# The four-block sum of a Strassen part formed ahead of the part's last z, converted in halves, and VectorE's weight work tied into an order of need

## The chip, the cores and the metric

The program runs on one core of one Trainium2 chip. The metric is the device time of one execution in microseconds (us). Five engines matter: TensorE (PE in the profile; PEld is its weight load), VectorE (DVE), ScalarE (ACT), GpSimd (POOL) and SyncE (SP), which issues most transfers.

## What is computed

A decoder trunk of two layers over 512 positions of width 1024. Each layer has a mixer and then the block that this change is about, a gated convolution block:

```python
def conv_ffn(h, w_in, conv_w, conv_b, w_out):
    z = causal_dwconv(h @ w_in, conv_w, conv_b)
    u, g = jnp.split(z, 2, axis=-1)
    return (jax.nn.gelu(g) * u) @ w_out
...
    for l in range(DEPTH):
        ...
        h = rms_norm(x, norm_ffn[l])
        x = x + conv_ffn(h, ffn_w_in[l], ffn_conv_w[l], ffn_conv_b[l], ffn_w_out[l])
```

The inner width is 2816, that is 22 tiles of 128 channels, each with a gate g and a value u.

## The kernel before

**Precision.** Every product is made of three float32r products: each operand is split into a high part (rounded copy) and a low part (the rest). For weights, ScalarE copies the raw weight `wraw` into `whi`, and VectorE subtracts, `wlo = wraw - whi`; `convert` (L256 to L278) does that, four of each being kept (`WB`), three raw tiles (`RAW`). `mm3` then runs `whi` by `yh`, `whi` by `yl`, `wlo` by `yh`, in that order.

**Parts.** A feed-forward block runs in three parts, `PARTS`: 8, 8 and 6 of its 22 tiles. In a part, TensorE first makes the up-projections (tile `up`, 24 matmuls of 512 columns each, g and u in turn for each tile); VectorE scales each result into `z` (L807), ScalarE and VectorE apply the convolution (`a`, L810, L812), ScalarE the GELU (`gg`), and VectorE multiplies into `y` (L828). Then comes the part's down-projection (tile `dn`), added into the residual tiles `X`.

**Strassen in the down-projection.** The two parts of 8 tiles in each layer, four in all, use seven products instead of eight (matmuls of 128x256). Their left operands are blocks of the weight for a pair of output tiles `dp` (0 to 3): `a` (plain blocks, raw tile `wraw`), `s` and `r` (sums, tiles `ws` and `wr`) and `b` (a plain block, `wb`). `stage` loads blocks of a pair into `ws`, `wr`, `wb` by SP, and adds further blocks on the way with accumulating transfers issued by POOL. `form` finishes the sums on VectorE: the two-block sum half of `s` (L251), and from it and `wraw` the four-block sum, the other half of `r` (L253). The right operands are `y`, differences of its blocks (`tt`) and their high and low parts `yh`, `yl` (L311, L846, L847).

**Order.** TensorE follows `PORDER`, written out by hand; a step such as `"30"` is product 3 of pair 0, 12 matmuls (`20-` is the first 9 of them and `20+` the last 3). Below, "step 30" is that entry. `LEFT` says which left operand a product uses: 1 and 2 the halves of `a`, 5 and 6 those of `s`, 3 and 7 those of `r` (3 the four-block sum), 4 `b`. `WORDER` is the order in which left operands are converted. After each product its result is added to or taken from `X` on VectorE (L910, L908; products 5, 7 and 4 subtract). Products 6, 7 and 4 of a pair go on accumulating in the bank of product 1, so step 40 cannot begin before VectorE has read out step 70.

`wnext` converts `AHEAD` = 3 items ahead of the one in use, so a part's last up-projection starts with a0, s0 and a1 under way, and r0 is formed at the first down step. `behind` orders two instructions on an engine without a wait. `hold` keeps weight work of ScalarE and VectorE behind the split of the part's last `y`, so r0's four-block sum and both its conversions come after it. The scheduler that places instructions decides the rest of each engine's order; each engine runs its queue strictly in that order.

Of the kernel before, what the change touches and what calls it, by code (L numbers as in the profile page):

```python
# [17 lines left out]
P = 128  # L18
# [56 lines left out]
LEFT = {1: ("a", 0), 2: ("a", 1), 5: ("s", 0), 6: ("s", 1), 3: ("r", 0), 7: ("r", 1), 4: ("b", 0)}  # L75
WORDER = "a0 s0 a1 r0 s1 b0 a2 r1 s2 b1 a3 r2 s3 b2 r3 b3".split()
BANK = {1: "mm", 6: "mm", 7: "mm", 4: "mm", 5: "s", 3: "s", 2: "tr"}
# [5 lines left out]
def tile_trunk(ctx: ExitStack, tc: tile.TileContext, xT, par, fpar, w_v, w_q, w_k, w_u, w_pool, w_po, w_ao,  # L83
# [130 lines left out]
    sums = {}  # L214
    last_split, hold = [None, None], [None, None]

# [20 lines left out]
    def form(kind, i):  # L237
        n = chunks[i][1]
        h = n // 2
        stage(i)  # L240
        s, r, b = sums[i]
        if kind == "a":
            follow = [k for k in pairs if k > i]
            if follow and pairs[i][2] < KD // 2 - 1:
                stage(min(follow))
            return raw_of(i), n
        if kind == "b":
            return b[:, :h], h
        a = raw_of(i)
        if kind == "s":  # L250
            behind(nc.vector.tensor_tensor(s[:, h:n], s[:, :h], a[:, :h], op=ALU.add), hold[1])  # L251
            return s[:, :n], n
        behind(nc.vector.tensor_tensor(r[:, :h], s[:, h:n], a[:, h:], op=ALU.add), hold[1])  # L253
        return r[:, :n], n

    def convert():  # L256
        kind, at = items[len(ready)]
        if kind != "plain":
            raw, n = form(kind, at)
            hi, lo = (wp.tile([P, 1024], F32R, name=t, bufs=WB)[:, :n] for t in ("whi", "wlo"))  # L260
            behind(nc.scalar.copy(hi, raw), hold[0])  # L261
            behind(nc.vector.tensor_tensor(lo, raw, f(hi), op=ALU.subtract), hold[1])  # L262
            ready.append((hi, lo, n))
            return
        n = chunks[at][1]
# [6 lines left out]
        for i in range(parts):  # L272
# [3 lines left out]
            if len(ready) == 2:  # L276
                early[:] = [h_, l_]
        ready.append((hi, lo, n))  # L278

    def wnext(n, ahead=AHEAD):  # L280
# [519 lines left out]
    def ffn(layer, norm, after, cuts=None):  # L800
        def conv(m):
            c0 = (layer * 2 * NF + m) * 4
# [3 lines left out]
            z = T("z")  # L806
            ins = nc.vector.tensor_tensor(z, ps, bc, op=ALU.mult)  # L807
            later_ops[1] = later_ops[1] or ins
            a = T("a")
            nc.scalar.activation(a, z, AF.Identity, scale=cw[2], bias=cw[3])  # L810
            for sh, w in ((1, cw[1]), (2, cw[0])):
                nc.vector.scalar_tensor_tensor(a[:, sh:], z[:, :S - sh], w, a[:, sh:], op0=ALU.mult, op1=ALU.add)  # L812
            return a
# [5 lines left out]
    def part(j0, n, strassen, conv, after, cuts):  # L819
        def big(tag, w, dt=F32):  # L820
            return cur["tp"].tile([P, w], dt, name=tag, tag=tag, bufs=cur["bufs"][tag])

        def gated(j, y):
            g = conv(NF + j)
            gg = T("gg")
            nc.scalar.activation(gg, g, AF.Gelu_apprx_tanh)  # L826
            u = conv(j)
            nc.vector.tensor_tensor(y, u, gg, op=ALU.mult)  # L828
# [19 lines left out]
        for i in range(half):  # L848
# [16 lines left out]
            if late:  # L865
                sub(t1, b[0], b[1])
                cut_of(t1, 3, 4)
            gated(j0 + 2 * i + 1, y[:, S:])
            cut_of(y[:, S:], 1, 3)
# [16 lines left out]
        for what in PORDER:  # L886
# [3 lines left out]
            while key not in left:  # L890
                left[todo.pop(0)] = wnext(None)
            wh, wl = left[key]
            whole, fresh = what[-1] not in "+-", not what.endswith("+")
            if m in (1, 5, 2) and fresh:
# [9 lines left out]
            for d, t in {1: ((0, h0),), 2: ((0, h0),), 5: ((1, h1),), 6: ((0, h1),), 3: ((0, h1),), 7: ((1, h1),),  # L904
                         4: ((1, h0),)}[m]:
                x = X[2 * dp + d][:, t]
                if d:
                    nc.vector.tensor_tensor(x, x, ps, op=ALU.subtract)  # L908
                else:
                    nc.vector.tensor_tensor(x, ps, x, op=ALU.add)  # L910
        pe["on"] = False
# [187 lines left out]
```

## Time and profile before

| | us |
|---|---|
| median of 3 runs (1076.84 to 1077.23) | 1076.91 |
| the profiled execution | 1078.23 |
| its span, first to last instruction | 1076.5 |
| TensorE busy in the span | 1065.2 |
| VectorE busy | 835.1 |
| ScalarE busy | 545.6 |
| granted TensorE clock, mean | 1.000 |

The profiled execution took 1.32 us longer than the median of the runs, and 1.7 us of its time lie outside its span. The busy shares overlap: TensorE is busy in 99% of the span, VectorE in 78%, ScalarE in 51%.

### The profile page before, as it was taken

Reading aid. Unit: us, or ns where it says so; the run is one execution under the profiler, and the core shown is the slowest. Engines: PE = TensorE matmul, PEld = TensorE weight load, DVE = VectorE, ACT = ScalarE, POOL = GpSimd, SP = SyncE. Lnnn points to the kernel's source line nnn. Section 1 sums busy time; section 2 is a strip of 40 time slices with the busy share of each in tenths; the row PEclk is TensorE's granted clock in tenths of the full one; section 3 lists DMA queues with packets and bytes.
Section 4 is the critical chain, followed back from the end, with each engine's and each line's share of the span. In section 5 each row is a group of like instructions: output and inputs, shape, how many; then the busy total and the mean of one; then the engine's idle time right before and its main releaser. Section 6 shows DMA issues by size and latency. Waiting matters only on the chain.

```text
span 1076.5 us, 14242 instructions
## 1 busy us (share of the span) xinstructions
PE 1065.2 (99%) x5456; PEld 907.7 (84%) x5456; DVE 835.1 (78%) x1278; ACT 545.6 (51%) x785; POOL 46.6 (4%) x62
## 2 busy tenths in 40 slices
PE   9999999999999999999999999999999999999998
PEld 7888888888998889888888888888888888898887
DVE  7678879988868898676787989568898678976762
ACT  6557766544434444444648895445444344434440
POOL 1031001000100000000000000010001000000000
PEclk9999999999999999999999999999999999999999
DMA  7232115532762315322333133375317632144222
GB/s 265 97 101 85 62 57 154 140 98 59 184 172 97 97 42 136 119 87 75 122 98 108 50 103 87 104 212 141 98 40 196 175 96 85 57 118 134 84 75 81
DMA packets 41893, 118.09 MB, mean 110 GB/s; under 512 B 4832, under 2 KB 5216, under 8 KB 41824
## 3 DMA queue, kind: packets, MB, share of 16 engines
q1 hardware_dynamic: 36432, 107.47, 31.5%
q0 software_dynamic: 4608, 8.39, 5.0%
q10 hardware_dynamic: 784, 1.31, 0.5%
q8 instruction: 43, 0.70, 0.3%
q14 instruction: 26, 0.21, 0.1%
HBM read 114.01 MB, written 2.10 MB: 108 GB/s over the span
## 4 chain that ended last, share of the span: by engine, by line
PE 96%; DVE 1%; DMA 1%; ACT 1%; issue 0%; SPq 0%; DVEq 0%
PE up L299 44%; PE dn L299 25%; PE tk L299 6%; PE xr L299 5%; PE gt L299 5%; PE po L299 2%; PE u L299 2%; PE ao L299 2%; PE gp L299 1%; PE av L299 1%; PE s L299 1%; PE tr L302 1%; DMA ws<-in_dram 1%; DVE wlo L262 0%; ACT whi L261 0%; PE tp L302 0%
## 5 line engine op out<-in xcount | busy, mean ns | idle before, releaser
L299 PE MATMUL up<-xl,whi 128*128 128x512 f32 x704 | 274.0, 389 | 0.0
L299 PE MATMUL up<-xh,whi 128*128 128x512 f32 x704 | 273.9, 389 | 0.0
L299 PE MATMUL up<-xh,wlo 128*128 128x512 f32 x704 | 273.9, 389 | 0.0
L274 ACT CAST whi<-wraw 128x1024 fp32r<-128x1024 f32 (+4 forms) x177 | 165.6, 941 | 153.8 <-PE up L299 56.0
L275 DVE TENSOR_TENSOR wlo<-wraw,whi 128x1024 fp32r<-128x1024 f32 (+4 forms) x177 | 193.4, 1096 | 34.0 <-ACT whi L274 32.0
L299 PE MATMUL dn<-yh,whi 128*128 128x256 f32 (+1 forms) x550 | 166.4, 303 | 3.5 <-ACT whi L261 2.5
L299 PE MATMUL dn<-yh,wlo 128*128 128x256 f32 (+1 forms) x550 | 165.2, 301 | 3.0 <-DVE wlo L262 3.0
L299 PE MATMUL dn<-yl,whi 128*128 128x256 f32 (+1 forms) x550 | 164.8, 300 | 0.0
L299 PEld LDWEIGHTS up<-xl,whi 128*128 128x128 f32 x704 | 132.1, 188 | 27.5
L299 PEld LDWEIGHTS up<-xh,whi 128*128 128x128 f32 x704 | 132.1, 188 | 27.4
L299 PEld LDWEIGHTS up<-xh,wlo 128*128 128x128 f32 x704 | 132.1, 188 | 27.3
L812 DVE SCALAR_TENSOR_TENSOR a<-z,fprm,a 128x510 f32<-128x510 f32 (+1 forms) x176 | 130.9, 747 | 2.4
L807 DVE TENSOR_TENSOR z<-up,rbc 128x512 f32<-128x512 f32 x88 | 60.4, 688 | 68.0 <-PE up L299 67.7
L299 PEld LDWEIGHTS dn<-yh,whi 128*128 128x128 f32 x550 | 105.1, 191 | 9.1 <-ACT whi L261 3.4
L299 PEld LDWEIGHTS dn<-yh,wlo 128*128 128x128 f32 x550 | 105.1, 191 | 7.3 <-DVE wlo L262 3.9
L299 PEld LDWEIGHTS dn<-yl,whi 128*128 128x128 f32 x550 | 105.1, 191 | 3.7
L311 ACT CAST yh<-y 128x512 fp32r<-128x512 f32 (+1 forms) x44 | 23.9, 543 | 116.5 <-DVE y L828 116.5
L810 ACT ACTIVATE a<-z,fprm 128x512 f32<-128x512 f32 x88 | 71.4, 814 | 9.9 <-DVE z L807 8.9
L826 ACT ACTIVATE gg<-a 128x512 f32<-128x512 f32 x44 | 27.8, 633 | 81.2 <-DVE a L812 76.8
L299 PE MATMUL dn<-yy,whi 128*128 128x512 f32 x160 | 49.2, 389 | 0.0
L233 POOL DMA_DIRECT2D ws<-in_dram x16 | 14.3, 893 | 756.0 <-DMA wr<-in_dram 376.9
L416 DVE TENSOR_TENSOR x<-dn,x 128x512 f32<-128x512 f32 (+1 forms) x23 | 15.4, 668 | 36.2 <-PE dn L299 36.2
(218 smaller groups left out, 1656.6 us busy)
## 6 DMA issues: line engine op xcount, KB each, us to landing
wraw<-in_dram SPq DMA_DIRECT2D x147, 512.0 KB, 3.5
wraw<-in_dram SPq DMA_DIRECT2D x16, 384.0 KB, 3.1
wraw<-in_dram SPq DMA_DIRECT2D x16, 320.0 KB, 2.8
ws<-in_dram SPq DMA_DIRECT2D x16, 256.0 KB, 3.3
wr<-in_dram SPq DMA_DIRECT2D x16, 256.0 KB, 4.0
wb<-in_dram SPq DMA_DIRECT2D x16, 256.0 KB, 4.0
ws<-in_dram POOLq DMA_DIRECT2D x16, 256.0 KB, 6.2
wr<-in_dram POOLq DMA_DIRECT2D x16, 256.0 KB, 4.9
```

The lines of the kernel that those rows point to most:

```text
L233: nc.gpsimd.dma_start(out=s[:, :h], in_=low[:, h:], accum_op=ALU.add)
L274: h_ = nc.scalar.copy(hi[:, c], raw[:, c])
L275: l_ = nc.vector.tensor_tensor(lo[:, c], raw[:, c], f(hi[:, c]), op=ALU.subtract)
L299: in_order(nc.tensor.matmul(*a, **k))
L302: in_order(nc.tensor.transpose(*a))
L311: last_split[:] = [nc.scalar.copy(hi, src), nc.vector.tensor_sub(lo, src, f(hi))]
L416: nc.vector.tensor_tensor(X[d][:, t], ps[:, t], X[d][:, t], op=ALU.add)
L807: ins = nc.vector.tensor_tensor(z, ps, bc, op=ALU.mult)
L810: nc.scalar.activation(a, z, AF.Identity, scale=cw[2], bias=cw[3])
L812: nc.vector.scalar_tensor_tensor(a[:, sh:], z[:, :S - sh], w, a[:, sh:], op0=ALU.mult, op1=ALU.add)
L826: nc.scalar.activation(gg, g, AF.Gelu_apprx_tanh)
```

## The change

In the last u tile of a Strassen part, `two_halves` forms r0's four-block sum on VectorE ahead of that tile's `z` (L295 of the new code), converts its first half (which step 30 needs) right after `z`, ScalarE's part ahead of `a` (L299, L300), and leaves the second half's high part to ScalarE behind `a` (L308) and its low part (L313, `rest_low`) to a place behind the read-out of step 60. There a2 and b0 follow, then the second half of s1's low part, whose first half is made at step 50 (`convert(whole=False)`). a2 and b0 change places in `WORDER`. Steps 10, 50, 11 and 30 get an `ahead` of their own, and step 11 starts the load of a2 and the staging of pair 3. `form` no longer holds the sums behind the split of `y`; two-block sums of pairs 2 and 3 are tied behind the low part of their own `a` instead. TensorE's order is unchanged: the same matmuls, in the same sequence.

```diff
--- before.py
+++ after.py
@@ -73,7 +73,7 @@
 QB = {1: 0, 2: 1, 3: 2, 5: 3, 7: 4, 6: 5, 4: 6}
 
 LEFT = {1: ("a", 0), 2: ("a", 1), 5: ("s", 0), 6: ("s", 1), 3: ("r", 0), 7: ("r", 1), 4: ("b", 0)}
-WORDER = "a0 s0 a1 r0 s1 b0 a2 r1 s2 b1 a3 r2 s3 b2 r3 b3".split()
+WORDER = "a0 s0 a1 r0 s1 a2 b0 r1 s2 b1 a3 r2 s3 b2 r3 b3".split()
 BANK = {1: "mm", 6: "mm", 7: "mm", 4: "mm", 5: "s", 3: "s", 2: "tr"}
 
 PORDER = "10 50 11 20- 21- 20+ 21+ 30 60 51 70 12 40 61 31 22 71 52 41 13 62 32 23 72 53 63 42 73 33 43".split()
@@ -212,7 +212,7 @@
         raws.append(raw)
 
     sums = {}
-    last_split, hold = [None, None], [None, None]
+    last_split, hold, low_a = [None, None], [None, None], {}
 
     def raw_of(i):
         while len(raws) <= i:
@@ -248,20 +248,25 @@
             return b[:, :h], h
         a = raw_of(i)
         if kind == "s":
-            behind(nc.vector.tensor_tensor(s[:, h:n], s[:, :h], a[:, :h], op=ALU.add), hold[1])
+            behind(nc.vector.tensor_tensor(s[:, h:n], s[:, :h], a[:, :h], op=ALU.add), low_a.get(i))
             return s[:, :n], n
-        behind(nc.vector.tensor_tensor(r[:, :h], s[:, h:n], a[:, h:], op=ALU.add), hold[1])
+        nc.vector.tensor_tensor(r[:, :h], s[:, h:n], a[:, h:], op=ALU.add)
         return r[:, :n], n
 
-    def convert():
+    def convert(prev=None, whole=True):
         kind, at = items[len(ready)]
         if kind != "plain":
             raw, n = form(kind, at)
             hi, lo = (wp.tile([P, 1024], F32R, name=t, bufs=WB)[:, :n] for t in ("whi", "wlo"))
             behind(nc.scalar.copy(hi, raw), hold[0])
-            behind(nc.vector.tensor_tensor(lo, raw, f(hi), op=ALU.subtract), hold[1])
+            c = n if whole else n // 2
+            ins = behind(nc.vector.tensor_tensor(lo[:, :c], raw[:, :c], f(hi[:, :c]), op=ALU.subtract), prev or hold[1])
+            if kind == "a" and pairs[at][2] > 1:
+                low_a[at] = ins
             ready.append((hi, lo, n))
-            return
+            if not whole:
+                return lambda b: behind(nc.vector.tensor_tensor(lo[:, c:], raw[:, c:], f(hi[:, c:]), op=ALU.subtract), b)
+            return ins
         n = chunks[at][1]
         raw = raw_of(at)
         if n == S and "shi" in cur["bufs"]:
@@ -276,6 +281,36 @@
             if len(ready) == 2:
                 early[:] = [h_, l_]
         ready.append((hi, lo, n))
+
+    rest = []
+
+    def two_halves():
+
+
+        kind, at = items[len(ready)]
+        assert kind == "r"
+        n = chunks[at][1]
+        h = n // 2
+        _, r, _ = sums[at]
+        total = nc.vector.tensor_tensor(r[:, :h], sums[at][0][:, h:n], raw_of(at)[:, h:], op=ALU.add)
+
+        def finish(z):
+            hi, lo = (wp.tile([P, 1024], F32R, name=t, bufs=WB)[:, :n] for t in ("whi", "wlo"))
+            high = nc.scalar.copy(hi[:, :h], r[:, :h])
+            low = behind(nc.vector.tensor_tensor(lo[:, :h], r[:, :h], f(hi[:, :h]), op=ALU.subtract), z)
+            ready.append((hi, lo, n))
+            rest[:] = [hi[:, h:], lo[:, h:], r[:, h:n]]
+            return high, low
+
+        return total, finish
+
+    def rest_high(prev):
+        behind(nc.scalar.copy(rest[0], rest[2]), prev)
+
+    def rest_low(prev):
+        hi, lo, raw = rest
+        rest[:] = []
+        return behind(nc.vector.tensor_tensor(lo, raw, f(hi), op=ALU.subtract), prev)
 
     def wnext(n, ahead=AHEAD):
         while len(ready) < min(used[0] + 1 + ahead, len(items)):
@@ -798,18 +833,23 @@
 
 
     def ffn(layer, norm, after, cuts=None):
-        def conv(m):
+        def conv(m, ahead=None):
             c0 = (layer * 2 * NF + m) * 4
             cw = [fprm[:, c0 + i:c0 + i + 1] for i in range(4)]
             ps = up_tile(norm, "up")
             bc = norm.bc
             z = T("z")
-            ins = nc.vector.tensor_tensor(z, ps, bc, op=ALU.mult)
+            total, finish = ahead() if ahead else (None, None)
+            ins = behind(nc.vector.tensor_tensor(z, ps, bc, op=ALU.mult), total)
             later_ops[1] = later_ops[1] or ins
+            high, low = finish(ins) if ahead else (None, None)
             a = T("a")
-            nc.scalar.activation(a, z, AF.Identity, scale=cw[2], bias=cw[3])
+            ins = behind(nc.scalar.activation(a, z, AF.Identity, scale=cw[2], bias=cw[3]), high)
+            if ahead:
+                rest_high(ins)
             for sh, w in ((1, cw[1]), (2, cw[0])):
-                nc.vector.scalar_tensor_tensor(a[:, sh:], z[:, :S - sh], w, a[:, sh:], op0=ALU.mult, op1=ALU.add)
+                behind(nc.vector.scalar_tensor_tensor(a[:, sh:], z[:, :S - sh], w, a[:, sh:], op0=ALU.mult,
+                                                      op1=ALU.add), low)
             return a
 
         for j0, n, strassen in PARTS:
@@ -820,11 +860,11 @@
         def big(tag, w, dt=F32):
             return cur["tp"].tile([P, w], dt, name=tag, tag=tag, bufs=cur["bufs"][tag])
 
-        def gated(j, y):
+        def gated(j, y, ahead=None):
             g = conv(NF + j)
             gg = T("gg")
             nc.scalar.activation(gg, g, AF.Gelu_apprx_tanh)
-            u = conv(j)
+            u = conv(j, ahead)
             nc.vector.tensor_tensor(y, u, gg, op=ALU.mult)
 
         if not strassen:
@@ -865,7 +905,7 @@
             if late:
                 sub(t1, b[0], b[1])
                 cut_of(t1, 3, 4)
-            gated(j0 + 2 * i + 1, y[:, S:])
+            gated(j0 + 2 * i + 1, y[:, S:], two_halves if late else None)
             cut_of(y[:, S:], 1, 3)
             if late:
                 hold[:] = list(last_split)
@@ -888,8 +928,14 @@
             kind, at = LEFT[m]
             key = kind + what[1]
             while key not in left:
-                left[todo.pop(0)] = wnext(None)
+                left[todo.pop(0)] = wnext(None, {"10": 3, "50": 2, "11": 2, "30": 1}.get(what, AHEAD))
             wh, wl = left[key]
+            if what == "50":
+                second = convert(whole=False)
+            if what == "11":
+                nxt = items[len(ready)][1]
+                raw_of(nxt)
+                stage(min(k for k in pairs if k > nxt))
             whole, fresh = what[-1] not in "+-", not what.endswith("+")
             if m in (1, 5, 2) and fresh:
                 bank[m, dp] = PS("dn", BANK[m])
@@ -905,9 +951,11 @@
                          4: ((1, h0),)}[m]:
                 x = X[2 * dp + d][:, t]
                 if d:
-                    nc.vector.tensor_tensor(x, x, ps, op=ALU.subtract)
+                    ins = nc.vector.tensor_tensor(x, x, ps, op=ALU.subtract)
                 else:
-                    nc.vector.tensor_tensor(x, ps, x, op=ALU.add)
+                    ins = nc.vector.tensor_tensor(x, ps, x, op=ALU.add)
+            if what == "60":
+                second(convert(convert(rest_low(ins))))
         pe["on"] = False
 
     phase("ffn0", z=3, a=4, gg=2, y=1, tt=1, yh=4, yl=4, ws=3, wr=2, wb=2)
```

VectorE's queue in the first Strassen part, about where the down-projection begins, before (names: `wlo<-wr,whi` is the low part of r0, `wr<-ws,wraw` the four-block sum, `x_73` to `x_80` the residual tiles):

```order
L828 TENSOR_TENSOR y<-a,gg 128x512
L910 TENSOR_TENSOR x_75<-dn,x_75 128x256
L846 TENSOR_TENSOR tt<-y 128x256
L311 TENSOR_TENSOR yl<-y,yh 128x512
L847 SCALAR_TENSOR_TENSOR tt<-tt,y 128x256
L253 TENSOR_TENSOR wr<-ws,wraw 128x512
L847 SCALAR_TENSOR_TENSOR tt<-tt,y 128x256
L910 TENSOR_TENSOR x_73<-dn,x_73 128x256
L910 TENSOR_TENSOR x_75<-dn,x_75 128x256
L262 TENSOR_TENSOR wlo<-wr,whi 128x1024
```

And after, from the last u tile's `z` on:

```order
L843 TENSOR_TENSOR z<-up,rbc 128x512
L300 TENSOR_TENSOR wlo<-wr,whi 128x512
L956 TENSOR_TENSOR x_73<-dn,x_73 128x256
L851 SCALAR_TENSOR_TENSOR a<-z,fprm,a 128x511
L851 SCALAR_TENSOR_TENSOR a<-z,fprm,a 128x510
L954 TENSOR_TENSOR x_74<-x_74,dn 128x256
L868 TENSOR_TENSOR y<-a,gg 128x512
L956 TENSOR_TENSOR x_75<-dn,x_75 128x256
L886 TENSOR_TENSOR tt<-y 128x256
L346 TENSOR_TENSOR yl<-y,yh 128x512
L887 SCALAR_TENSOR_TENSOR tt<-tt,y 128x256 x2
L956 TENSOR_TENSOR x_73<-dn,x_73 128x256
```

The four-block sum and the 1024-column low part of r0 are gone from behind `y`; a 512-column low part now stands right behind `z`.

A little further on VectorE, before, from the last low part of the right operands (`yl<-tt,yh`) on:

```order
L311 TENSOR_TENSOR yl<-tt,yh 128x768
L262 TENSOR_TENSOR wlo<-ws,whi 128x1024
L262 TENSOR_TENSOR wlo<-wb,whi 128x512
L910 TENSOR_TENSOR x_73<-dn,x_73 128x256
L253 TENSOR_TENSOR wr<-ws,wraw 128x512
L910 TENSOR_TENSOR x_73<-dn,x_73 128x256
L262 TENSOR_TENSOR wlo<-wraw,whi 128x1024
L908 TENSOR_TENSOR x_76<-x_76,dn 128x256
L251 TENSOR_TENSOR ws<-ws,wraw 128x512
L908 TENSOR_TENSOR x_74<-x_74,dn 128x256
```

And after:

```order
L346 TENSOR_TENSOR yl<-tt,yh 128x768
L263 TENSOR_TENSOR wlo<-ws,whi 128x512
L956 TENSOR_TENSOR x_73<-dn,x_73 128x256 x2
L313 TENSOR_TENSOR wlo<-wr,whi 128x512
L263 TENSOR_TENSOR wlo<-wraw,whi 128x1024
L263 TENSOR_TENSOR wlo<-wb,whi 128x512
L268 TENSOR_TENSOR wlo<-ws,whi 128x512
L954 TENSOR_TENSOR x_76<-x_76,dn 128x256
L954 TENSOR_TENSOR x_74<-x_74,dn 128x256
L263 TENSOR_TENSOR wlo<-wr,whi 128x1024
L251 TENSOR_TENSOR ws<-ws,wraw 128x512
```

s1's low part is split and its rest moved behind b0's; r0's second half comes behind the read-out of steps 30 and 60 (`x2`); the read-outs of steps 51 and 70 (`x_76`, `x_74`) now stand behind four low parts, and sums of later pairs (L253, L251) have moved out from among them.

The same four-block sum in its new place on VectorE, among the up-projections (after):

```order
L251 TENSOR_TENSOR ws<-ws,wraw 128x512
L280 TENSOR_TENSOR wlo<-wraw,whi 128x1024
L851 SCALAR_TENSOR_TENSOR a<-z,fprm,a 128x511
L295 TENSOR_TENSOR wr<-ws,wraw 128x512
L851 SCALAR_TENSOR_TENSOR a<-z,fprm,a 128x510
L843 TENSOR_TENSOR z<-up,rbc 128x512
L251 TENSOR_TENSOR ws<-ws,wraw 128x512
```

It was not there before; the rest of that stretch is unchanged but for a sum of pair 2 (L251) that leaves it.

ScalarE's queue at the start of the down-projection, before:

```order
L826 ACTIVATE gg<-a 128x512
L810 ACTIVATE a<-z,fprm 128x512
L311 CAST yh<-y 128x512
L261 CAST whi<-wr 128x1024
L311 CAST yh<-tt 128x768
```

And after:

```order
L866 ACTIVATE gg<-a 128x512
L299 CAST whi<-wr 128x512
L847 ACTIVATE a<-z,fprm 128x512
L308 CAST whi<-wr 128x512
L346 CAST yh<-y 128x512
L346 CAST yh<-tt 128x768
```

r0's high part is now two casts of 512 on either side of `a`, ahead of the cast of `y`.

## Rows read from the trace of the kernel before

**Rows 1.** The page: busy us of the matmuls and the weight loads, and others.

```profile
PE 1065.2 (99%) x5456; PEld 907.7 (84%) x5456; DVE 835.1 (78%) x1278; ACT 545.6 (51%) x785; POOL 46.6 (4%) x62
```

**Rows 2.** Who waited for whom, TensorE alone: total us, times, longest.

```profile
PE dn L299 <- DVE wlo L262: 3.0, 4, 0.8
PE dn L299 <- ACT whi L261: 2.5, 4, 0.6
PE dn L299 <- DVE x L908: 0.8, 1, 0.8
```

**Rows 3.** Timeline, TensorE, first Strassen part: start, duration, idle before in brackets.

```profile
266.01 0.28 PE L299 MATMUL dn<-yh,whi 128*128 128x256 f32 x1
...
267.32 0.28 PE L299 MATMUL dn<-yh,wlo 128*128 128x256 f32 x1
...
273.08 0.28 PE L299 MATMUL dn<-yh,wlo 128*128 128x256 f32 x1
274.00 0.39 PE L299 MATMUL dn<-yh,whi 128*128 128x256 f32 x1 [0.64 <-ACT whi L261]
274.22 0.28 PE L299 MATMUL dn<-yl,whi 128*128 128x256 f32 x1
275.26 0.39 PE L299 MATMUL dn<-yh,wlo 128*128 128x256 f32 x1 [0.76 <-DVE wlo L262]
275.48 0.28 PE L299 MATMUL dn<-yh,whi 128*128 128x256 f32 x1
```

**Rows 4.** Timeline, VectorE, the same stretch.

```profile
266.21 0.69 DVE L807 TENSOR_TENSOR z<-up,rbc 128x512 f32<-128x512 f32 x1 [1.38 <-PE up L299]
267.65 0.42 DVE L910 TENSOR_TENSOR x<-dn,x 128x256 f32<-128x256 f32 x1 [0.74 <-PE dn L299]
267.99 1.53 DVE L812 SCALAR_TENSOR_TENSOR a<-z,fprm,a 128x511 f32<-128x511 f32 x2
...
272.14 0.68 DVE L253 TENSOR_TENSOR wr<-ws,wraw 128x512 f32<-128x512 f32 x1
...
273.07 0.75 DVE L910 TENSOR_TENSOR x<-dn,x 128x256 f32<-128x256 f32 x2
273.98 1.23 DVE L262 TENSOR_TENSOR wlo<-wr,whi 128x1024 fp32r<-128x1024 f32 x1
275.12 0.95 DVE L311 TENSOR_TENSOR yl<-tt,yh 128x768 fp32r<-128x768 f32 x1
...
277.12 0.68 DVE L262 TENSOR_TENSOR wlo<-wb,whi 128x512 fp32r<-128x512 f32 x1
277.73 0.42 DVE L910 TENSOR_TENSOR x<-dn,x 128x256 f32<-128x256 f32 x1
```

**Rows 5.** Timeline, ScalarE, the same stretch.

```profile
272.90 1.05 ACT L261 CAST whi<-wr 128x1024 fp32r<-128x1024 f32 x1 [1.80 <-PE dn L299]
...
275.53 0.61 ACT L261 CAST whi<-wb 128x512 fp32r<-128x512 f32 x1
```

**Rows 6.** Timeline, VectorE, up-projections ahead of that part.

```profile
244.45 0.69 DVE L807 TENSOR_TENSOR z<-up,rbc 128x512 f32<-128x512 f32 x1 [1.48 <-PE up L299]
```

**Rows 7.** Timeline, third Strassen part: VectorE and, behind it, TensorE.

```profile
817.92 0.69 DVE L251 TENSOR_TENSOR ws<-ws,wraw 128x512 f32<-128x512 f32 x1 [1.50 <-DMA ws<-in_dram]
...
819.00 0.38 PE L299 MATMUL dn<-yh,whi 128*128 128x256 f32 x1 [0.82 <-DVE x L908]
```

**Rows 8.** Timeline, first part, step 41: VectorE's read-out, then TensorE.

```profile
290.38 0.41 DVE L908 TENSOR_TENSOR x<-x,dn 128x256 f32<-128x256 f32 x1
...
290.96 0.34 PE L299 MATMUL dn<-yh,whi 128*128 128x256 f32 x1
291.13 0.28 PE L299 MATMUL dn<-yl,whi 128*128 128x256 f32 x1
```

**Rows 9.** The page, transfers of `wr`: KB each, median us to landing.

```profile
wr<-in_dram SPq DMA_DIRECT2D x16, 256.0 KB, 4.0
...
wr<-in_dram POOLq DMA_DIRECT2D x16, 256.0 KB, 4.9
```

## The prediction

> **What bounds the kernel now.** TensorE does: it is busy in 1065.2 us, 99% of the span [rows 1], and its granted clock is 1.000, the higher of its two levels, so only TensorE's waits can be won or lost. The second view is the list of those waits [rows 2]. Three lines of it stand in the down-projections: four waits for a low part made at L262, four for a high part made at L261, one for a read-out at L908. Four is the number of Strassen parts. The reader is to see from the count that it is one place, visited four times.
>
> The third view is TensorE's own timeline of the first part [rows 3]. The down-projection starts at 266.01, and up to 273.08 its 60 matmuls start every 0.12 us (7.07 us over 59 steps). Those 60 are steps 10, 50, 11 and both pieces of 20 and 21. Step 30 should follow at 273.20; it comes at 274.00, its second matmul at 274.22, its third, the first to read the low weights, at 275.26, and only from 275.48 does the beat return. 273.08 to 275.48 is 2.40 us for four steps that take 0.48: **1.92 us lost a part, 7.68 in four**. Note that the idle times in brackets (0.64 and 0.76) show less than that: each restart costs some 0.26 more, 0.10 of it in the next matmul (0.22 in place of 0.12).
>
> Why step 30 waits is read on the other engines. VectorE forms r0's four-block sum at 272.14, behind the split of `y`; ScalarE's cast of 1024 follows at 272.90, when the sum has ended, and VectorE's low part at 273.98, when the cast has [rows 4, 5]. Sum, cast and low part are a chain of 3.1 us that begins 1 us before its result is wanted. Yet VectorE idled 1.38 us before the last `z` and 0.74 after it, waiting for TensorE. The inputs were there: the same raw tile had served s0's sum long before.
>
> The one wait for L908 is in the third part. VectorE sits 1.50 us before a sum of pair 3 (L251) until POOL's accumulating transfer into `ws` has landed; the read-out of step 70 is queued behind it, and TensorE begins step 40 at 819.00 after 0.82 idle [rows 7]. With 0.26 for the restart, 1.08 us.
>
> **The change part by part.** I write the beat as 0.12 from 266.01: step 30 is due at 273.20, 60 at 274.64, 51 at 276.08, 70 at 277.51, 12 at 278.95, 40 at 280.39. Prices, start to start: 1.14 us for a low part of 1024 (273.98 to 275.12), 0.61 for one of 512 (277.12 to 277.73), 0.34 for a read-out [rows 4].
>
> *The sum made early* (0.61 more on VectorE among the up-projections). It lies in front of a `z` for which VectorE idled 1.48 us [rows 6], and a sum of pair 2 leaves the same stretch a little later, so it costs nothing. Without that idle time it would put off the `z` by 0.6 us, at most that much for TensorE.
>
> *r0's first half.* ScalarE's cast (0.61, by that of `wb` in [rows 5]) needs the weight buffer of the last u tile, free when TensorE ends that tile, the moment `z` starts at 266.21. It ends at about 266.8, before `z` does at 266.9, so `a` is not held up. VectorE's half low part runs from 266.9 to 267.5, inside the 0.74 idle before the read-out at 267.65 [rows 4]. So both halves of what step 30 reads are there 5.7 us early, and the two waits go. ScalarE's second cast falls into the time in which it waited for `y`.
>
> *Step 60* needs the 768-column low part of `tt` at 275.72, for its last three matmuls. Before, that began at 275.12, behind the 1024 low part of r0; without sum and low part in front it begins when the two read-outs of 273.07 are done, about 273.75, and ends by 274.7.
>
> *s1's first half* follows, 274.6 to 275.3, for step 51 at 276.08.
>
> *r0's second half* stands behind the read-out of step 60. Step 60's last matmul starts at 275.96; a read-out starts 0.33 later (267.32 to 267.65 in [rows 3, 4]), so at 276.29; the low part runs from 276.63 to 277.31. Step 70 reads it with its third matmul at 277.75: 0.44 to spare, fixed against TensorE's own progress.
>
> *a2 and b0*: 276.63 + 0.61 + 1.14 = 278.38 for a2, wanted at 279.19; b0 to 278.99, wanted at 280.63.
>
> *The place that is late next.* Then come s1's second half, to 279.60, and the read-outs of 51 and 70, to 279.94 and 280.35. Step 40, due at 280.39, must wait for that last read-out. This is 0.04 of margin. The nearest row is step 41 before: its read-out ended at 290.79, 0.17 ahead of the matmul at 290.96, and the next came 0.17 later instead of 0.12 [rows 8], so a near miss already costs 0.05. A full restart costs 0.10 in the next matmul and 0.16 before it [rows 3]. Bounds for step 40: nothing, if the read-outs run 0.2 earlier than I count; 0.7, if one more operation of 0.61 gets ahead of it. I take 0.10, between the near miss and a full restart and nearer the first: **0.40 in four parts**.
>
> *The third part's 1.08* go in any case: pair 3's `ws` is now free when s0's low part is made, in the up-projections, so that transfer is issued ahead of the down-projection, and its sum stands some fourteen places later in VectorE's queue.
>
> *What the splits add.* Two halves take 1.22 in place of 1.14, 0.08 twice a part; both are counted in the times above. The Trainium skill, in Perfetto Trace Analysis, section Optimizing Scalar/DVE Operations, speaks against splitting: each VectorE instruction on SBUF carries some 60 ns of access time, so larger operations win where the engine is saturated, while breaking them up helps where an unsaturated engine holds up another. By its figure the two extra instructions cost an estimated 0.12 us a part; if all of that fell on TensorE, the new price would be 0.48 in place of my 0.40 and the sum below 1069.95. VectorE is not saturated here, it idled before and behind `z` [rows 4], which by the same section is the case for breaking up; that an earlier first half frees TensorE no row shows yet.
>
> **Sum** against the profiled execution: 1078.23 - 7.68 - 1.08 + 0.40 = 1069.87. The median of the runs is 1.32 below that execution, and since only one of four like places had the late transfer, the runs may well have been without it. So for the median, 1076.91 - 7.28 = 1069.6 without it, 1068.5 with; I take the middle, **1069.1**.
>
> **The rivals.**
> *Step 40 becomes the wait.* For it: the margin of 0.04, and four queued low parts ahead of the read-out. Against it: it needs another 0.6 of delay. At the bound, 0.7 a part, 1076.91 - 7.68 + 2.8 = 1072.0.
> *Only one of the two waits goes*: the halved low part misses its gap, or the wait moves to step 51, because s1's cast is held by ScalarE's longer queue. That leaves about half, 0.96 a part: 1073.1. The 5.7 and 0.8 us of margin speak against it.
> *The change does nothing*: the early sum waits for data and blocks `z`, the two prices cancel; 1076.9. Against it, s0's sum reads the same raw tile ahead of it without waiting there.
> *Slower: the accumulating transfer of r2 comes too late.* Its buffer is r0's. Before, it was freed at 275.2; now by r0's second half at 277.3. Plain transfer 4.0 and POOL's accumulating one 4.9 [rows 9]: landing at 286.2. Step 32 is due 228 matmuls after the start, at 293.3; the read-out of step 52, a low part of 1.14 and a cast of 1.05 stand before it, so the landing must come by 290.6. Each us beyond is lost in every part, but it takes 4.4 to begin, and (7.8 + 2.2) / 4 = 2.5 more to be slower by over 0.2%: 1079.1 at that point. The same transfers are needed either way, and fewer of them now run together with it.
>
> **How the numbers follow.** Chances: the forecast 0.80, step 40 0.09, half of it 0.04, no change 0.04, slower 0.03. 0.2% (2.15 us) is about what a measurement of this kernel can tell from no change; the first three cases are all beyond it, so faster 0.93, same 0.04, slower 0.03. The lower bound is all waits gone from the runs at no new price: 1076.91 - 7.68 - 1.08 = 1068.15, put at 1067.8 for the matmuls that lose 0.05 to 0.08 at other near misses; the upper is the step-40 rival, 1072.0.
>
> **What would show it.** Right: step 30's first three matmuls start 0.12 apart, about 60 beats after the part begins; the waits for the low and high part of r0 are gone from the list; a part's down-projection takes little over its 336 beats, 40.3 us; the half low part starts within 0.1 of the end of `z`. Wrong: a wait of TensorE for a read-out (now L954) at step 40, of over 0.2 in each part; VectorE waiting for a transfer in the new queue; a cast of ScalarE that starts late and delays `a`. If all waits are gone and the time falls by less than 6 us, the lost 1.92 was misread.

## The result, and the profile after

| | before | after |
|---|---|---|
| median of the runs, us | 1077.07 (4 runs, 1076.84 to 1077.83) | 1069.65 (4 runs, 1069.56 to 1069.76) |
| the profiled execution | 1078.23 | 1069.59 |
| its span | 1076.5 | 1067.8 |

The ratio after to before is 0.9930, with a 95% interval of 0.9913 to 0.9947: faster by 7.4 us. The forecast was 1069.1, with a range of 1067.8 to 1072.0.

The page's row of busy times after, the counterpart of [rows 1]:

```profile
PE 1062.4 (99%) x5456; PEld 907.3 (85%) x5456; DVE 835.3 (78%) x1286; ACT 547.4 (51%) x789; POOL 46.6 (4%) x62
```

TensorE has as many matmuls as before; its busy time fell by 2.8 us and the span by 8.7, so most of the gain is idle time that is gone. VectorE has eight instructions more, two halvings in each of four parts. Two views follow: TensorE's waits, to be read against [rows 2], and, from the chain of work that ended last, the first and the last of the four down-projections of the Strassen parts (start, duration, matmuls):

```profile
PE wm L334 <- DVE sc L975: 1.1, 1, 1.1
PE tk L334 <- DVE xh L369: 0.6, 1, 0.6
PE tr L337 <- DVE ptl L635: 0.2, 1, 0.2
```

```profile
265.99 40.53 PE dn L334 x336
...
925.55 40.53 PE dn L334 x336
```

All three waits of the down-projection are gone; the three that are left lie in other stages (one of them, 0.6 at `tk`, was not in the list before; the first Strassen part comes after it and starts no later for it). In all four parts the 336 matmuls form one unbroken piece of the chain, of 40.53 or 40.54 us (a piece begins where the row of the last up-projection ends, 0.17 after the part's first matmul starts). TensorE's timeline of the first part, around step 30 and around step 40, answers to [rows 3]:

```profile
265.82 0.28 PE L334 MATMUL dn<-yh,whi 128*128 128x256 f32 x1
...
272.90 0.28 PE L334 MATMUL dn<-yh,wlo 128*128 128x256 f32 x1
273.02 0.28 PE L334 MATMUL dn<-yh,whi 128*128 128x256 f32 x1
273.14 0.28 PE L334 MATMUL dn<-yl,whi 128*128 128x256 f32 x1
273.26 0.28 PE L334 MATMUL dn<-yh,wlo 128*128 128x256 f32 x1
...
280.10 0.28 PE L334 MATMUL dn<-yh,wlo 128*128 128x256 f32 x1
280.26 0.35 PE L334 MATMUL dn<-yh,whi 128*128 128x256 f32 x1
280.46 0.28 PE L334 MATMUL dn<-yl,whi 128*128 128x256 f32 x1
```

The part now starts at 265.82; 60 matmuls later, at 273.02, step 30 begins, and its three first matmuls keep the beat of 0.12. Before, 2.40 us lay between the same two neighbours, 273.08 and 275.48. At step 40 two gaps are 0.16 and 0.20 in place of 0.12: 0.12 us lost, with no idle time shown.

VectorE in the same stretch, to be read against [rows 4]:

```profile
266.02 0.69 DVE L843 TENSOR_TENSOR z<-up,rbc 128x512 f32<-128x512 f32 x1 [1.64 <-PE up L334]
266.63 0.68 DVE L300 TENSOR_TENSOR wlo<-wr,whi 128x512 fp32r<-128x512 f32 x1
...
273.56 0.95 DVE L346 TENSOR_TENSOR yl<-tt,yh 128x768 fp32r<-128x768 f32 x1
274.42 0.69 DVE L263 TENSOR_TENSOR wlo<-ws,whi 128x512 fp32r<-128x512 f32 x1
...
276.10 0.42 DVE L956 TENSOR_TENSOR x<-dn,x 128x256 f32<-128x256 f32 x1 [0.65 <-PE dn L334]
276.44 0.68 DVE L313 TENSOR_TENSOR wlo<-wr,whi 128x512 fp32r<-128x512 f32 x1
277.04 1.22 DVE L263 TENSOR_TENSOR wlo<-wraw,whi 128x1024 fp32r<-128x1024 f32 x1
278.17 0.68 DVE L263 TENSOR_TENSOR wlo<-wb,whi 128x512 fp32r<-128x512 f32 x1
278.77 0.68 DVE L268 TENSOR_TENSOR wlo<-ws,whi 128x512 fp32r<-128x512 f32 x1
279.38 0.74 DVE L954 TENSOR_TENSOR x<-x,dn 128x256 f32<-128x256 f32 x2
```

The reader is to see the half low part in the gap that VectorE had behind `z`, and at the end the queue that now stands ahead of step 40: four low parts without idle time, then the read-outs of steps 51 and 70 (`x2`), which end at 280.12, 0.14 ahead of step 40's first matmul.

### The profile page after: what moved, and what is told of

Its sections match the earlier page's. It is cut to its first block, busy times and chain, and to the rows that moved or that the text cites. A ratio compares the mean times of both kernels' runs of the same rounds, so it can differ in the third digit from the quotient of the medians.

```text
span 1067.8 us, 14275 instructions
## 1 busy us (share of the span) xinstructions
PE 1062.4 (99%) x5456; PEld 907.3 (85%) x5456; DVE 835.3 (78%) x1286; ACT 547.4 (51%) x789; POOL 46.6 (4%) x62
## 4 chain that ended last, share of the span: by engine, by line
PE 94%; DVE 4%; ACT 1%; DMA 0%; issue 0%; SPq 0%
PE up L334 45%; PE dn L334 26%; PE tk L334 6%; PE gt L334 5%; PE xr L334 3%; PE po L334 2%; PE u L334 2%; PE ao L334 2%; PE av L334 1%; PE s L334 1%; PE tr L337 1%; PE gp L334 1%; DVE a L1038 1%; DVE h L1019 1%; DVE wlo L280 0%; PE tp L337 0%
```

## The experiments

Each time in the table is the median of all runs of a kernel. The kernel before ran beside them, with medians of 1077.21 beside e1 to e4 (21 runs), 1076.96 beside e5 to e8 (21) and 1077.01 beside e9 and e10 (12).

| run | what it is | median us (lowest to highest, runs) | ratio to before, 95% |
|---|---|---|---|
| e1_sum_only | before + the early sum | 1078.14 (1077.76 to 1078.66, 11) | 0.9998 to 1.0015 |
| e2_halves_only | before + r0 in halves | 1079.56 (1079.13 to 1080.23, 11) | 1.0010 to 1.0028 |
| e3_s1_whole | after, s1's low part whole | 1069.25 (1069.18 to 1069.28, 4) | 0.9909 to 0.9936 |
| e4_40_later | after, step 40 behind 61 | 1069.24 (1069.13 to 1069.38, 4) | 0.9909 to 0.9936 |
| e5_r0_whole | after, r0 whole | 1069.45 (1069.28 to 1069.70, 5) | 0.9917 to 0.9942 |
| e6_both_whole | after, nothing halved | 1071.30 (1070.97 to 1071.37, 5) | 0.9934 to 0.9958 |
| e7_order_only | after, r0's sum late again | 1076.85 (1076.71 to 1077.32, 11) | 0.9989 to 1.0007 |
| e8_ws4 | before, four `ws` buffers | 1076.89 (1076.78 to 1077.06, 11) | 0.9990 to 1.0008 |
| e9_one_tie | e1 + a2's low part behind step 60's read-out | 1074.61 (1074.02 to 1075.04, 8) | 0.9965 to 0.9985 |
| e10_best | e3 + step 41 behind 13 | 1069.17 (1069.02 to 1069.41, 5) | 0.9912 to 0.9940 |

**The early sum alone.** In the kernel before, the sum is formed ahead of the last z; everything else is left.

```diff
-        behind(nc.vector.tensor_tensor(r[:, :h], s[:, h:n], a[:, h:], op=ALU.add), hold[1])
+        if i not in formed:
+            behind(nc.vector.tensor_tensor(r[:, :h], s[:, h:n], a[:, h:], op=ALU.add), hold[1])
...
+            total = ahead() if ahead else None
+            ins = behind(nc.vector.tensor_tensor(z, ps, bc, op=ALU.mult), total)
```

> The kernel before, with one part of the change: r0's four-block sum stands ahead of the part's last z; both conversions stay whole (1024 columns) and stay behind the split of y. Theory (the place of the sum gives the gain, the halves are not needed for it): ScalarE's cast of r0 starts as soon as the cast of y is done, about 271.1 instead of 272.90 in the first part, ends at 272.15; VectorE's low part runs 272.15 to 273.3, just ahead of step 30's third matmul at 273.44. Nearly all of the 1.92 us a part goes: 1076.9 - 4 x 1.8 = 1069.7 us, range 1069.2 to 1070.5. Rival (the halves carry the gain): the whole low part misses 273.44 by 0.3 or more, a wait for the low part made at the converting line shows in all four parts with at least 0.6 a part: 1072.0 us or more. Third possibility: the sum of pair 2, which moves from 254.0 to the place ahead of the last z, waits for data and puts off z: slower than 1076.9.

It gains nothing: 1078.14 beside 1077.21, with an interval that includes no change. My theory fell. TensorE's waits in the down-projection, and its timeline where most is lost:

```profile
PE dn L311 <- DVE x L923: 4.8, 4, 1.2
PE dn L311 <- DVE wlo L274: 1.1, 3, 0.4
```

```profile
278.20 0.28 PE L311 MATMUL dn<-yh,wlo 128*128 128x256 f32 x1
279.67 0.38 PE L311 MATMUL dn<-yh,whi 128*128 128x256 f32 x1 [1.19 <-DVE x L923]
279.89 0.28 PE L311 MATMUL dn<-yl,whi 128*128 128x256 f32 x1
```

Step 30's wait fell from 1.92 to between 0.35 and 0.65 a part, but a new wait of 1.45 (1.69 between three starts that should take 0.24) stands behind it. Counted from step 30, 279.67 is the first matmul of step 70. A smaller loss, 0.27 to 0.29 in each part, lies at the eleventh and twelfth matmul of step 60 and is in no list of waits. The eleventh reads the low part of `tt`, which ends at 276.49 behind r0's and s1's whole low parts:

```profile
276.26 0.28 PE L311 MATMUL dn<-yh,whi 128*128 128x256 f32 x1
276.55 0.39 PE L311 MATMUL dn<-yl,whi 128*128 128x256 f32 x1
276.77 0.28 PE L311 MATMUL dn<-yh,wlo 128*128 128x256 f32 x1
```

Step 70 goes on accumulating in the bank that step 60 filled, so it needs step 60's read-out. VectorE's and ScalarE's timelines tell why that is late:

```profile
277.01 0.75 DVE L923 TENSOR_TENSOR x<-dn,x 128x256 f32<-128x256 f32 x2
278.05 1.23 DVE L274 TENSOR_TENSOR wlo<-wraw,whi 128x1024 fp32r<-128x1024 f32 x1 [0.29 <-ACT whi L273]
279.20 0.42 DVE L923 TENSOR_TENSOR x<-dn,x 128x256 f32<-128x256 f32 x1
```

```profile
276.97 1.05 ACT L273 CAST whi<-wraw 128x1024 fp32r<-128x1024 f32 x1 [1.42 <-PE dn L311]
```

The scheduler now puts a2's low part (278.05) ahead of step 60's read-out (279.20); in the kernel before it stood behind it. That low part waits for a2's cast, and the cast begins at 276.97, released by TensorE, 0.20 after step 60's last matmul started (276.77): its weight buffer is free only then. So step 60's read-out, which could start soon after that last matmul, stands behind 0.29 of idle time and 1.2 us of low part.

The third possibility that I had put down came in part too: a two-block sum (of pair 3, not 2) stands ahead of the last z, waits for POOL's transfer and puts off z by 0.7 us against [rows 4]:

```profile
265.65 0.69 DVE L251 TENSOR_TENSOR ws<-ws,wraw 128x512 f32<-128x512 f32 x1 [1.72 <-DMA ws<-in_dram]
...
266.92 0.68 DVE L820 TENSOR_TENSOR z<-up,rbc 128x512 f32<-128x512 f32 x1
```

**The halves alone.** In the kernel before, `convert` makes r0's cast and low part in two pieces.

```diff
+            first = kind == "r" and pairs[at][2] == 0
+            for c in (slice(0, n // 2), slice(n // 2, n)) if first else (slice(0, n),):
+                behind(nc.scalar.copy(hi[:, c], raw[:, c]), hold[0])
+                behind(nc.vector.tensor_tensor(lo[:, c], raw[:, c], f(hi[:, c]), op=ALU.subtract), hold[1])
```

> The kernel before, with the other part of the change alone: r0's cast and low part in two halves of 512, the four-block sum and both conversions still behind the split of y. Theory (the place of the sum decides, halves give only the difference of the durations): the sum still ends at 272.9, so step 30 gets its first high half at about 273.5 instead of 273.95 and its low half at about 274.2 instead of 275.2; about 0.9 us a part is won and about 1.0 stays: 1076.9 - 3.7 = 1073.2 us, range 1072.3 to 1074.3, with both waits still in the list. Rival (the halves carry the gain): both waits gone, 1070 us or less.

Measured 1079.56, slower than before. The waits expected at step 30 are there, and were sized rightly: in the first part 273.02 to 274.57 is 1.55 for four steps that take 0.48, so 1.07.

```profile
273.02 0.28 PE L301 MATMUL dn<-yh,wlo 128*128 128x256 f32 x1
273.46 0.38 PE L301 MATMUL dn<-yh,whi 128*128 128x256 f32 x1 [0.17 <-ACT whi L263]
273.68 0.28 PE L301 MATMUL dn<-yl,whi 128*128 128x256 f32 x1
274.35 0.38 PE L301 MATMUL dn<-yh,wlo 128*128 128x256 f32 x1 [0.39 <-DVE wlo L264]
274.57 0.28 PE L301 MATMUL dn<-yh,whi 128*128 128x256 f32 x1
```

But the same new wait for the read-out at step 70 came with them, as TensorE's list of waits shows:

```profile
PE dn L301 <- DVE x L912: 4.7, 4, 1.2
```

4 x (1.07 + 1.45 - 1.92) = +2.4, and 1079.56 is 2.35 above the kernel before beside it. In both runs a shorter wait at step 30 came with one at step 70.

**The order alone.** The changed kernel with r0's sum and conversions behind the split of y.

```diff
-            gated(j0 + 2 * i + 1, y[:, S:], two_halves if late else None)
+            gated(j0 + 2 * i + 1, y[:, S:])
...
-        nc.vector.tensor_tensor(r[:, :h], s[:, h:n], a[:, h:], op=ALU.add)
+        behind(nc.vector.tensor_tensor(r[:, :h], s[:, h:n], a[:, h:], op=ALU.add), hold[1])
...
-                second(convert(convert(rest_low(ins))))
+                second(convert(convert(ins)))
```

> The changed kernel without the early sum: r0's four-block sum, cast and low part (whole) are behind the split of the last y as in the kernel before; the order of need behind steps 50 and 60, the early load of a2 and staging of pair 3, and a2 ahead of b0 stay. Theory (both parts are needed, the early sum gives the 1.92 a part and the order only keeps it): step 30 waits as before, for the high and then the low part, 1.9 us a part; steps 70 and 40 do not wait: 1069.65 + 7.7 - 0.5 = 1076.8 us, range 1076.3 to 1077.5. Rival (the order by itself gives half or more): 1073.5 us or less.

1076.85, as the theory said. The waits are those of [rows 2] to the digit, and none for a read-out:

```profile
PE dn L334 <- DVE wlo L263: 3.0, 4, 0.8
PE dn L334 <- ACT whi L261: 2.5, 4, 0.6
```

So neither the early sum nor the order is worth anything by itself, and the early sum, with r0's halves, adds 7.2 us to the order: the early sum removes the loss, the order keeps it from coming back. The early sum and the halves together, without the order, were not run.

**One tie added to the early sum.** The run with the early sum alone, with a2's low part behind step 60's read-out. Its conversion is called for at step 60 instead of step 30; its cast still begins 0.20 after step 60's last matmul (276.50 and 276.30).

```diff
-                left[todo.pop(0)] = wnext(None)
+                left[todo.pop(0)] = wnext(None, 2 if what == "30" else AHEAD)
...
+            if what == "60":
+                hold[1] = ins
+                convert()
+                hold[1] = None
```

> The run with the early sum alone (1078.14 us), with one tie more: a2's low part is placed behind the read-out of step 60 on VectorE instead of ahead of it. Theory (that run lost its gain because step 70 waits for the read-out of step 60, and this stands behind a2's low part, whose cast waits for the weight buffer that step 60 itself frees): the read-out of step 60 now comes about 0.8 us earlier, behind two other read-outs and one sum; step 70's 1.45 us a part shrink to 0.5 or less, 4 x 0.95 to 4 x 1.45 less: 1072.3 to 1074.4 us. Waits at step 30 (0.64 a part) stay. Rival (step 70 waits for something else, such as r0's low part): no change, 1077.8 us or more.

1074.61, 3.5 us below the run without the tie, 0.2 above the range expected. TensorE at step 70:

```profile
277.73 0.28 PE L311 MATMUL dn<-yh,wlo 128*128 128x256 f32 x1
278.28 0.38 PE L311 MATMUL dn<-yh,whi 128*128 128x256 f32 x1 [0.27 <-DVE x L923]
278.50 0.28 PE L311 MATMUL dn<-yl,whi 128*128 128x256 f32 x1
```

Its loss fell from 1.45 to 0.53 a part; 4 x 0.92 = 3.7 accounts for the 3.5 us. The cause of the wait at step 70 is shown. What this kernel still loses against the changed one lies at step 70 (a sum of 0.6 us stands ahead of that read-out), at step 30 (0.24 to 0.65 a part) and at step 60 (0.27 or 0.28): pair 3's sum still waits for its transfer ahead of z (1.48 us of idle time in the first part), and the conversions come after y.

**The halves, taken out of the changed kernel.** r0 whole, s1 whole, both whole:

```diff
-            high = nc.scalar.copy(hi[:, :h], r[:, :h])
-            low = behind(nc.vector.tensor_tensor(lo[:, :h], r[:, :h], f(hi[:, :h]), op=ALU.subtract), z)
+            high = nc.scalar.copy(hi, r[:, :n])
+            low = behind(nc.vector.tensor_tensor(lo, r[:, :n], f(hi), op=ALU.subtract), z)
...
-                second = convert(whole=False)
+                convert()
```

> The changed kernel, with r0 in one piece: its cast of 1024 columns ahead of the last a, its low part of 1024 right behind the last z, nothing of r0 left behind step 60. Theory (what counts is that the sum is early and that the later work stands in an order of need; the halves only spread it): the last a starts about 0.1 us later and the last y about 0.5 later, which TensorE does not feel (in the run with the early sum alone y was 0.7 later); behind step 60 0.6 us of VectorE's queue is gone, so step 40's 0.12 goes as well: 1069.2 us, range 1069.0 to 1069.7. Rival (the halves are needed): a later y makes the second piece of step 20 or step 60 wait, 0.3 a part or more: 1070.5 us or more.

> The changed kernel, with s1's low part in one piece of 1024 where its first half stood, and nothing behind b0's. Theory (step 40's lost 0.12 to 0.13 a part comes from the read-out of step 70, which ends at 280.12 behind s1's second half, too close ahead of the matmul at 280.26): the read-out ends about 0.6 us earlier, step 40 starts on the beat, 4 x 0.12 = 0.5 us less: 1069.15 us, range 1069.0 to 1069.4. Rival (the whole low part is needed too late or delays r0's second half): step 51 or 70 waits, 0.3 us a part or more: 1070.5 us or more. No effect (1069.65, within 0.1) would say that step 40's lost time has another cause.

> The changed kernel with no halves at all: r0 in one piece ahead of y, s1's low part in one piece. With the early sum and the order of need but without halving it tells whether the run with the early sum alone failed for want of halves or for want of the order. Theory (for want of the order): 1069.2 us, at most 1070.4, if the low part of tt, now behind a later y, comes 0.3 a part too late for step 60's last matmuls. Rival (for want of halves): a wait of more than 1 us a part comes back, at step 30 or 70: 1074 us or more.

With r0 whole 1069.45, with s1 whole 1069.25: neither halving is needed by itself. s1's costs 0.4 us; for r0's, 0.2 with overlapping runs, the times settle no cost. The timelines with r0 whole show step 40's 0.12 gone from all four parts, as expected, and 0.04 at the end of step 20 and 0.02 or 0.03 at step 60 in its place. With s1 whole, the read-outs of 51 and 70 come 0.57 us earlier, on VectorE's timeline, and step 40's matmuls are back on the beat (280.13, 280.25, 280.37):

```profile
278.81 0.74 DVE L954 TENSOR_TENSOR x<-x,dn 128x256 f32<-128x256 f32 x2
```

With both whole one halving is missed: 1071.30, above the 1070.4 that I allowed. The place was the one expected, its size larger, 0.43 a part instead of 0.3: r0's whole low part puts off the last y, s1's whole low part stands ahead of the low part of tt, and step 60's eleventh matmul waits. VectorE's and then TensorE's timeline:

```profile
273.86 1.23 DVE L263 TENSOR_TENSOR wlo<-ws,whi 128x1024 fp32r<-128x1024 f32 x1 [0.19 <-ACT whi L261]
275.00 0.95 DVE L345 TENSOR_TENSOR yl<-tt,yh 128x768 fp32r<-128x768 f32 x1
```

```profile
275.56 0.28 PE L333 MATMUL dn<-yh,whi 128*128 128x256 f32 x1
276.01 0.39 PE L333 MATMUL dn<-yl,whi 128*128 128x256 f32 x1 [0.16 <-DVE yl L345]
276.23 0.28 PE L333 MATMUL dn<-yh,wlo 128*128 128x256 f32 x1
```

It is still 5.7 us faster than before: the early sum and the order carry most of the gain without any halving, and one of the two halvings adds the rest.

**Step 40's lost 0.12.** TensorE's order changed in one place:

```diff
-... 60 51 70 12 40 61 31 ...
+... 60 51 70 12 61 40 31 ...
```

> The changed kernel, with step 40 behind step 61 in TensorE's order instead of ahead of it, nothing else. Theory (step 40's lost 0.12 to 0.13 a part is a wait for the read-out of step 70): with 12 more matmuls (1.44 us) between them that time is given back, 4 x 0.12 = 0.5 us: 1069.15 us, range 1069.0 to 1069.4. Rival: step 61 now stands where 40 stood and reads s1's or r's operands that come as late, so the same 0.1 a part or more appears there: 1069.65 us or more. If this and the run with s1 whole differ by more than 0.3, the read-out is not the cause.

1069.24, and with s1 whole 1069.25: moving the read-out earlier and moving the matmul later give back the same 0.4 us, and in both timelines step 40 is on the beat. Step 40's loss is the wait for the read-out of step 70.

**The same for step 41**, on top of s1 whole:

> The changed kernel with s1's low part in one piece (1069.25 us by itself) and step 41 behind step 13 in TensorE's order. Theory (the 0.05 that step 41 loses in each part is the read-out of step 71, too close ahead of it): with 12 more matmuls between, it goes too, 4 x 0.05 less: 1069.05 us, range 1068.9 to 1069.25. Rival: step 13 or a later step reads a weight that now comes too late: 1069.5 us or more.

The lost 0.05 at step 41 is gone from the timelines of all four parts; of each down-projection's near misses only 0.07 to 0.08 at step 43 is left. The median, 1069.17, is 0.08 below that with s1 whole, but the runs overlap (up to 1069.41), so the times alone don't settle it. Both beat the change, by 0.4 to 0.5 us.

**The third part's late transfer.** The kernel before with room for a fourth two-block sum:

```diff
-    phase("ffn0", z=3, a=4, gg=2, y=1, tt=1, yh=4, yl=4, ws=3, wr=2, wb=2)
+    phase("ffn0", z=3, a=4, gg=1, y=1, tt=1, yh=4, yl=4, ws=4, wr=2, wb=2)
```

(and `ffn1` likewise)

> The kernel before with four buffers for the two-block sums instead of three (and one for gg instead of two, to make room): the transfers for pair 3 no longer wait for the first pair's buffer. All else, the late sum of r0 too, as before. The executions of the kernel before fall into two groups, 1076.8 to 1077.2 and 1077.7 to 1078.2 us. Theory (the upper group has the late accumulating transfer of the third part, 1.08 us): the upper group is gone, all runs within 1076.6 to 1077.3, median 1076.9; the waits for the converting lines stay at 5.5 us in the list. Rival (the two groups have another cause): both are there again, about 1 us apart.

All eleven runs lie within 1076.78 to 1077.06, as the theory said. In its trace the waits for the low and high part of r0 are as in [rows 2], the one for a read-out is gone. The 21 runs of before that stand beside e1 to e4 fall into eleven at 1076.81 to 1077.21 and ten at 1077.68 to 1078.21; but of the 21 beside this one only one lies in the upper group (1078.22; the others end at 1077.53), and of the 12 beside e9 and e10 three (1077.71, 1077.99, 1078.22), so the times alone do not prove that the transfer makes the upper group. These three sets ran on three different chips, and the chip may play a part. For it speaks that the profiled execution of before, with the wait of 1.08, took 1078.23 and that of this kernel, without it, 1076.89; of the 1.34 between them 0.25 was there before the first Strassen part began (266.01 and 265.76). No run of before in the lower group has a trace, so the cause of the two groups stays likely, not shown.

## Why the prediction was right

**The loss at step 30** (1.92 a part, 7.68) was read rightly and went whole. Order alone against the changed kernel, which has 0.12 a part more at step 40, gives 1076.85 - 1069.65 + 0.48 = 7.68; that it agrees to the last digit is chance, as each median's runs spread over 0.2 to 0.6 us. Between the two profiled executions the time fell by 8.64, where the sum had 8.36; 0.19 of the difference was there when the first part began.

**Each place in the queue** came where the sum had it, 0.18 to 0.23 earlier, of which 0.19 is the part's start (265.82 instead of 266.01): the 768-column low part at 273.56 (273.75 predicted), s1's first half at 274.42 (274.6), r0's second half at 276.44 (276.63). VectorE's idle time ahead of the earlier z, 1.48 in [rows 6], fell by the price of the sum:

```profile
244.26 0.69 DVE L843 TENSOR_TENSOR z<-up,rbc 128x512 f32<-128x512 f32 x1 [0.90 <-PE up L334]
```

**Step 40** was named as the place that is late next, at 0.10 a part; it lost 0.12 or 0.13 in each part. That the price came so near is partly luck: the read-out of step 70 ended 0.10 ahead of the beat (280.12 and 280.22), not the 0.04 of the sum, and even this larger margin cost more than the 0.10 put on the smaller one.

**The third part's 1.08** went as described: the plain transfer into pair 3's `ws` is now issued at 789.43, ahead of that part's down-projection, where before it was issued at 808.56, within it, and pair 3's sum starts without idle time. What was off is how much of it the median held. The three runs shown (1076.84 to 1077.23) are of the lower group, and the branch without the late transfer, 1069.6, is the one that was measured, 1069.65; I took the middle, 0.55 too low. The fourth run of before, 1077.83, is of the upper group.

**The slower rival** did not begin: r2's cast waits for TensorE, not for its transfer.

```profile
287.65 1.05 ACT L261 CAST whi<-wr 128x1024 fp32r<-128x1024 f32 x1 [0.44 <-PE dn L334]
```

But the argument that the transfers would run less together was not borne out: the accumulating ones into `wr` took 6.1 us to landing (median) instead of 4.9 in [rows 9].

```profile
wr<-in_dram POOLq DMA_DIRECT2D x16, 256.0 KB, 6.1
```

**What the prediction did not see** is which part of the change does what. It put the gain down to the early sum and the halves, and priced the ties only as places in a queue. The runs showed that either halving can go (1069.25 and 1069.45 against 1069.65), while leaving out both costs 1.65 us (1071.30). They showed the ties to be worth all that the early sum wins: without them, in the early sum alone, the scheduler's own order turns most of step 30's wait into one at step 70. The forecast held because it took the order of the changed kernel as built, instruction by instruction, and not because its account of the causes was whole.

**The splits.** Step 40 lost 4 x 0.12 = 0.5 us in four parts, which is nearer to 0.48 than to my 0.40. That 0.48 was an estimate from the Trainium skill (Perfetto Trace Analysis, section Optimizing Scalar/DVE Operations, some 60 ns for each extra instruction). The rows after come near its figure: a split costs 0.07 start to start, 0.60 twice against 1.13. But the runs put the loss at step 40 down to something else, the whole 0.6 us of s1's second half ahead of a read-out, so the two agree in size only.

## What to carry to other kernels

When a wait on the bounding engine is taken away, its next wait is set by the order of the queues behind it: before the edit, write out which read-out and which buffer the following steps need, and pin those ahead of work that isn't due yet. An operation whose own input comes late (a2's low part here, whose cast waits for a weight buffer to come free) must not stand in a strict queue ahead of something that the bounding engine needs sooner. Split operations only where a place needs it: here either split could be taken out again without a loss, but not both.

## What the runs showed of the hardware

With these matmuls of 128x256, a wait of TensorE cost 0.25 to 0.27 us more than the idle time shown, for idle times of 0.16 to 1.19: 0.16 shown and 0.43 lost (both whole), 0.17 and 0.42, 0.39 and 0.65 (halves alone), 0.27 and 0.53 (one tie), 1.19 and 1.45 (early sum alone). About 0.10 of it lies in the matmul after the one that waited, which comes 0.22 later instead of 0.12. The other 0.16 is how the profile counts: a matmul's row lasts 0.28, the next one on the beat starts 0.12 after it, and idle time counts only from the end of the row. So a wait that the list shows as 0.27 cost 0.53, twice as much.

For the same reason a matmul that starts up to 0.16 late shows no idle time at all. Step 60 lost 0.27 to 0.29 in each part of the early sum alone with at most 0.03 between the end of one row (276.54) and the start of the next (276.55), and no entry in the list of waits.

A read-out that ended 0.14 us ahead of the matmul that needed it, with no wait in the list, still cost 0.12 at step 40; one that ended 0.17 ahead cost 0.05 at step 41 [rows 8].
